# RG-LRU loop of a hybrid diffusion block: width-4 convolution and gates on the products in PSUM, zero columns around the context, another order of the products

## The chip, the cores and the metric

The kernel runs on one core of one Trainium2 chip. The metric is the device time of one execution in microseconds.

## The reference

One layer works on 512 latent tokens (`x`) and 256 context tokens (`ctx`), 1024 channels each, in fp32. The part that matters here is the recurrent branch of the token mixer. Its input `x_r` is a projection of the normalised and modulated tokens. It goes through a depthwise convolution of width 4 (latent and context tokens apart, with zero padding of one token before and two after), and then for each of two directions through gates and a linear recurrence that runs over the context first:

```
xr = dwconv1d(xr, lru_conv_w, (1, 2)) + lru_conv_b
for d in range(2):
    r = sigmoid(heads(xr) @ w_r[d] + b_r[d]);  i = sigmoid(heads(xr) @ w_i[d] + b_i[d])
    log_a = -8 * r * softplus(-lam[d]);        a = exp(log_a)
    u = sqrt(-expm1(2 * log_a)) * (i * xr)
    h = scan(h = a * h + u), latent tokens start from the last context state; d = 1 runs backwards
    rec = h if d == 0 else rec + h
```

`rec` times a GeLU gate is projected, merged with a Conformer branch (GLU, depthwise convolution of width 31, LayerNorm, projection), and followed by an output projection and a gated ConvFFN.

## The kernel before, in words

Channels lie on the partitions, tokens on the columns. The 1024 channels of a branch are 8 blocks of 128. Every fp32 operand of a product is split into a high and a low float32r part, and a product is three matmuls (`mm3`, L134 to 137). A product of a block over 512 tokens (`block`, L143) is 24 matmuls. Weights come by DMA from the SP queue in a fixed order (`queue`, `W`, L94 to 132). ScalarE makes a weight's high part (L123), GpSimd its low part (L124). `W` converts two entries ahead of the one that is asked for. The order on every engine is the order of the calls in the program: the schedule is manual, and each engine's queue is strictly in order.

The loop over the blocks (L640 to 699) is software pipelined. In iteration b TensorE computes x_r of block b, the gates of block b-1, and the g and v products of block b+1 for the GLU. VectorE and GpSimd do the scans of block b-2. The tiles of the products lie in PSUM under tags: `mm2` (two buffers of 1024 columns, for x_r, the gates, and gelu blocks 4 and 5), `mm1` (two of 512, for g, v and the other gelu blocks) and `cv` (two of 512). A buffer is given out again in rotation, and the first writer waits until all readers of the tile before have run.

- `xr_post` (L539): ScalarE copies x_r from PSUM into a zero-padded SBUF tile `xrp` (latent at 1, context at 515; L541, L542), and makes the first tap `xw` from it (L545). VectorE adds two taps over 770 columns (L547), with a fill after each, and the last tap in two pieces (L550, L552) into `xc`.
- `xc_split` (L556): high part on ScalarE, low part on GpSimd (helper `split`, L140, L141).
- `gates` (L562): two products, of r and of i, of direction d. `gates_act` (L583): ScalarE takes the tanh of both from PSUM into SBUF tiles `tg` (L580), then a = exp (L589) and a second tanh (L590). GpSimd squares a into `e2` (L592; the page and the trace call it `e`).
- `gates_dve` (L595): the input-gate product (L598) and the r product (L600), both from SBUF.
- `scans_act` (L602): square roots (L605), which need another activation table. `scans` (L607): the scan product (L610), by VectorE for direction 0 and by GpSimd for direction 1; three scans (L614 to 616); the sum of the directions on GpSimd (L617).
- `fill(n)` (L532) hands out n operations of the width-31 convolution (`conv31`, L484, taps at L500) to VectorE. What the loop leaves is done by the next stage, before the LayerNorm's mean (L788 to 792).
- `ada_step` (L289) adds a product of the adaLN modulation, two per iteration in b = 2 to 5, from tiles loaded in the same iteration (L673 to 676). `decay_rates` (L370) is a chain of small GpSimd operations before the loop.

Before the loop the products of block 0 are made into `psA` and `psC`, `psg` is g of block 2 and `ps1` is x_r of block 1 (L473 to 476). After it (L701 to 722) follow the gates of block 7, the scans of blocks 6 and 7 and the gelu blocks (`gt_block`, `gt_act`, L622 to 629), then the stage of the gb and yb products (L750).

## Time and profile before

| | us |
|---|---|
| median of three runs | 909.12 |
| the three runs | 909.12, 909.26, 906.13 |
| span of the profiled execution, first to last instruction | 906.8 |
| TensorE matmul busy | 860.2 |
| VectorE busy | 723.3 |
| GpSimd busy | 476.6 |
| ScalarE busy | 440.3 |

The profile gives the span of one execution, not its time as the runs count it; that is the span and what lies around it. Engines are PE (TensorE), DVE (VectorE), ACT (ScalarE), POOL (GpSimd) and SP. A row names line, engine, operation, and "out<-in" by the program's names. The time of the RG-LRU loop is from about 73 to 276 us. PEclk is TensorE's granted clock as a share of full speed. Matmuls overlap, so the time of a product is read from start to start. A "[1.34 <-ACT ...]" behind a row is the engine's idle time before it and what ended it.

### The profile page before, as it was taken

How to read it: one execution, taken by the hardware profiler on the slowest of the kernel's cores; microseconds unless marked ns; L12 is line 12 of the kernel's file. 1: busy time of each engine (PE TensorE's matmuls, PEld its weight loads, DVE VectorE, ACT ScalarE, POOL GpSimd, SP SyncE). 2: the span in 40 equal slices, each digit the busy share in tenths (PEclk: the TensorE clock that was granted, in tenths of full speed). 3: DMA queues.
4: the chain of work that ended last, by engine and by line, in shares of the span. 5: the costliest groups of instructions: out<-in, count | busy, mean ns of one | idle time of the engine just before them, and what ended most of it. 6: DMA issues, size and time to landing. Idle time of an engine off the chain costs nothing.

```text
span 906.8 us, 11008 instructions
## 1 busy us (share of the span) xinstructions
PE 860.2 (95%) x4114; PEld 692.0 (76%) x4114; DVE 723.3 (80%) x952; ACT 440.3 (49%) x625; POOL 476.6 (53%) x263
## 2 busy tenths in 40 slices
PE   7999989888989999999898999999999999999997
PEld 6787777766867768887676788988888888888775
DVE  4387999999999888885888334699999898899314
ACT  5285656654678455422654245544443443435322
POOL 2229667555766499955344213254554564547810
PEclk9999999988999989999999899999999999999999
DMA  9942133213212222324425322133333333233402
GB/s 351 367 195 82 35 128 128 94 52 111 82 47 94 93 71 96 113 94 163 160 82 177 124 108 70 48 105 116 124 101 122 116 119 116 91 130 116 163 1 93
DMA packets 31397, 105.97 MB, mean 117 GB/s; under 512 B 3441, under 2 KB 3569, under 8 KB 31345
## 3 DMA queue, kind: packets, MB, share of 16 engines
q1 hardware_dynamic: 31344, 105.29, 33.8%
q8 instruction: 32, 0.52, 0.2%
q14 instruction: 21, 0.16, 0.1%
HBM read 103.17 MB, written 2.10 MB: 116 GB/s over the span
## 4 chain that ended last, share of the span: by engine, by line
PE 60%; DVE 29%; ACT 5%; DMA 3%; issue 3%; POOL 1%; SPq 0%; DVEq 0%; ACTq 0%; POOLq 0%
PE up_ps L136 8%; PE up_ps L135 8%; PE up_ps L137 8%; DVE cv L500 6%; DVE xw L547 3%; DVE tg L598 3%; DVE e L600 3%; DVE ggb L294 2%; PE y_ps L135 2%; PE y_ps L137 2%; PE y_ps L136 2%; PE gb_ps L137 2%; DVE rec L615 2%; PE gb_ps L135 1%; PE gb_ps L136 1%
## 5 line engine op out<-in xcount | busy, mean ns | idle before, releaser
L124 POOL TENSOR_TENSOR wlo<-raw,whi 128x1024 fp32r<-128x1024 f32 (+1 forms) x126 | 314.4, 2508 | 200.5 <-ACT whi L123 198.0
L1016 DVE SCALAR_TENSOR_TENSOR cv<-zall,P,cv 128x512 f32<-128x512 f32 x240 | 161.7, 741 | 0.2
L500 DVE SCALAR_TENSOR_TENSOR cv<-glu,P,cv 128x512 f32<-128x512 f32 x208 | 141.5, 746 | 0.0
L123 ACT ACTIVATE whi<-raw 128x1024 fp32r<-128x1024 f32 (+1 forms) x129 | 129.5, 1023 | 16.4 <-issue 10.9
L135 PE MATMUL up_ps<-Ahi,whi 128*128 128x512 f32 (+1 forms) x352 | 131.9, 375 | 0.0
L136 PE MATMUL up_ps<-Alo,whi 128*128 128x512 f32 (+1 forms) x352 | 131.8, 374 | 0.0
L137 PE MATMUL up_ps<-Ahi,wlo 128*128 128x512 f32 (+1 forms) x352 | 131.7, 374 | 0.0
L136 PEld LDWEIGHTS up_ps<-Alo,whi 128*128 128x128 f32 x352 | 66.1, 188 | 13.2
L137 PEld LDWEIGHTS up_ps<-Ahi,wlo 128*128 128x128 f32 x352 | 66.1, 188 | 13.2
L135 PEld LDWEIGHTS up_ps<-Ahi,whi 128*128 128x128 f32 x352 | 66.1, 188 | 13.1
L1002 POOL TENSOR_TENSOR acl<-fo,ach 128x512 fp32r<-128x512 f32 x20 | 26.0, 1301 | 85.5 <-ACT ach L999 85.5
L1016 DVE SCALAR_TENSOR_TENSOR cv<-zall,P,cc 128x512 f32<-128x512 f32 x40 | 43.1, 1104 | 21.1 <-ACT cc L990 21.1
L988 ACT ACTIVATE zall<-up_ps 128x512 f32<-128x512 f32 x40 | 23.7, 593 | 63.3 <-PE up_ps L137 63.3
L999 ACT ACTIVATE ach<-fo 128x512 fp32r<-128x512 f32 x20 | 12.7, 633 | 66.8 <-DVE fo L998 66.8
L294 DVE SCALAR_TENSOR_TENSOR ggb<-wa,sT,ggb 128x1024 f32<-128x1024 f32 (+1 forms) x35 | 43.7, 1249 | 0.4
L135 PE MATMUL gate_ps<-xh,whi 128*128 128x512 f32 x64 | 24.1, 376 | 17.8 <-ACT xrp L542 17.7
L547 DVE SCALAR_TENSOR_TENSOR xw<-xrp,P,xw 128x770 f32<-128x770 f32 x16 | 33.7, 2107 | 2.1 <-ACT xw L545 2.0
L135 PEld LDWEIGHTS gate_ps<-xh,whi 128*128 128x128 f32 x64 | 13.0, 203 | 22.7 <-ACT xrp L542 20.1
L598 DVE SCALAR_TENSOR_TENSOR tg<-tg,xc 128x768 f32<-128x768 f32 x16 | 30.2, 1885 | 0.0
L605 ACT ACTIVATE e<-e 128x768 f32<-128x768 f32 x16 | 13.5, 846 | 33.9 <-DVE e L600 33.8
L617 POOL TENSOR_TENSOR rec<-rec,tg 128x512 f32<-128x512 f32 x7 | 9.2, 1311 | 36.6 <-DVE tg L616 36.6
L580 ACT ACTIVATE tg<-gate_ps,P 128x768 f32<-128x768 f32 x32 | 27.4, 898 | 2.0 <-PE gate_ps L137 1.8
(386 smaller groups left out, 2245.9 us busy)
## 6 DMA issues: line engine op xcount, KB each, us to landing
raw<-in_win_dram SPq DMA_DIRECT2D x48, 512.0 KB, 3.4
raw<-in_wup_dram SPq DMA_DIRECT2D x40, 512.0 KB, 3.3
wa<-in_wada_dram SPq DMA_DIRECT2D x24, 512.0 KB, 5.5
raw<-in_wdn_dram SPq DMA_DIRECT2D x22, 512.0 KB, 3.3
wa<-in_wadq_dram SPq DMA_DIRECT2D x16, 512.0 KB, 9.3
raw<-in_wpl_dram SPq DMA_DIRECT2D x8, 512.0 KB, 3.2
raw<-in_wpc_dram SPq DMA_DIRECT2D x8, 512.0 KB, 3.3
raw<-in_wout_dram SPq DMA_DIRECT2D x8, 512.0 KB, 3.3
```

Of the source, the lines that this page charges most:

```text
L123: S.activation(out=flat(hl[0]), in_=flat(t), func=AF.Copy)
L124: eng.tensor_sub(flat(hl[1]), flat(t), flat(hl[0]))
L135: PE.matmul(o, lh, rh, start=first, stop=False)
L136: PE.matmul(o, lh, rl, start=False, stop=False)
L137: PE.matmul(o, ll, rh, start=False, stop=last)
L294: V.scalar_tensor_tensor(out=acc, in0=w, scalar=s, in1=acc, op0=ALU.mult, op1=ALU.add)
L500: V.scalar_tensor_tensor(out=cv[b] if k else glu[:, b, 0:T], in0=glu[:, b, k:k + T], scalar=col("dw31", 31 * b + k, 1), in1=cv[b], op0=ALU ...
L547: V.scalar_tensor_tensor(out=xw, in0=pad[:, k:k + 770], scalar=lw[k], in1=xw, op0=ALU.mult, op1=ALU.add)
L580: S.activation(out=t, in_=lru[b, d, q][:, 0:TA], func=AF.Tanh, scale=0.5, bias=hb[:, 16 * q + i:16 * q + i + 1])
L598: V.scalar_tensor_tensor(out=ti, in0=ti, scalar=1.0, in1=xcs[b][0], op0=ALU.add, op1=ALU.mult)
L600: V.scalar_tensor_tensor(out=e2, in0=e2, scalar=1.0, in1=tr, op0=ALU.add, op1=ALU.mult)
L1016: V.scalar_tensor_tensor(out=o, in0=zz[i, s][:, k // 3:k // 3 + GH, k % 3:k % 3 + GW], scalar=col("dw9", 9 * (i + FW * (1 - s)) + k, 1), i ...
```

## The change

The context's products are made over 262 columns, with three zero columns on either side of `chi` and `clo`, so that the x_r product lies in PSUM with its own zero padding. The copies into `xrp` go. ScalarE makes the second tap with the bias straight from PSUM (`xr_act`), and VectorE adds the other three with PSUM as one operand (`xr_post`). The tanh of the gates, and the second tanh of r, are written in place in PSUM. The input-gate product goes into a new tile `u`, and the r product reads PSUM. The backward and forward scans write into `e2`. Gate weights get buffers of their own (`gw`). In the loop the four gate products are taken apart: r of direction 0 after the context product; i of direction 0 and r of direction 1 after g (or a gelu block); i of direction 1 after v. The part behind the loop is reordered in the same way, and squares for block 7 move from VectorE to GpSimd. The loop's fills are 82 (90 before), and those behind it 6 (10 before). Comments are dropped too.

```diff
+TP = TC + 6
...
-    chi = ph.tile([128, NB, TC], F32R, name="chi")
-    clo = ph.tile([128, NB, TC], F32R, name="clo")
+
+    chi = ph.tile([128, NB, TP], F32R, name="chi")
+    clo = ph.tile([128, NB, TP], F32R, name="clo")
+    for t in (chi, clo):
+        for sl in (slice(0, 3), slice(3 + TC, TP)):
+            G.memset(t.bitcast(F32)[:, :, sl] if hasattr(t, "bitcast") else t[:, :, sl], 0.0)
     w0h = ph.tile([128, NB, 128], F32R, name="w0h")
     w0l = ph.tile([128, NB, 128], F32R, name="w0l")
+
+    def gate_dst():
+        return tuple(ph.tile([128, 4, 128], F32R, tag=f"gw{n}", bufs=2, name=f"gw{n}") for n in "hl")
...
-        queue(("gate", b - 1), wgate[b - 1], [4, 128])
+        queue(("gate", b - 1), wgate[b - 1], [4, 128], gate_dst)
...
-        split(h, chi[:, k:k + 2, :], clo[:, k:k + 2, :])
+        split(h, chi[:, k:k + 2, 3:3 + TC], clo[:, k:k + 2, 3:3 + TC])
...
-    block(psA[:, T:TA], ready[0], chi, clo)
+    block(psA[:, T:T + TP], ready[0], chi, clo)
...
-    def xr_post(b, ps, n=1):
-        pad = xrp[b % 2]
-        S.activation(out=pad[:, 1:1 + T], in_=ps[:, 0:T], func=AF.Copy)
-        S.activation(out=pad[:, 515:515 + TC], in_=ps[:, T:TA], func=AF.Copy)
+
+    def xr_act(b, ps):
+        xw = pl.tile([128, 771], F32, tag="xw", bufs=1, name="xw")
+        S.activation(out=xw, in_=ps[:, 0:771], func=AF.Identity, scale=col("lru_w", 4 * b + 1, 1),
+                     bias=col("lru_b", b, 1))
+        return xw
+
+    def xr_post(b, ps, xw, n=1):
         lw = [col("lru_w", 4 * b + k, 1) for k in range(4)]
-        xw = pl.tile([128, 770], F32, tag="xw", bufs=1, name="xw")
-        S.activation(out=xw, in_=pad[:, 0:770], func=AF.Identity, scale=lw[0], bias=col("lru_b", b, 1))
-        for k in (1, 2):
-            V.scalar_tensor_tensor(out=xw, in0=pad[:, k:k + 770], scalar=lw[k], in1=xw, op0=ALU.mult, op1=ALU.add)
-            fill(n)
+        V.scalar_tensor_tensor(out=xw[:, 1:771], in0=ps[:, 0:770], scalar=lw[0], in1=xw[:, 1:771], op0=ALU.mult, op1=ALU.add)
+        fill(n)
+        V.scalar_tensor_tensor(out=xw, in0=ps[:, 1:772], scalar=lw[2], in1=xw, op0=ALU.mult, op1=ALU.add)
+        fill(n)
         xc = pl.tile([128, TA], F32, tag="xc", name="xc")
-        V.scalar_tensor_tensor(out=xc[:, 0:T], in0=pad[:, 3:3 + T], scalar=lw[3], in1=xw[:, 0:T],
-                               op0=ALU.mult, op1=ALU.add)
-        V.scalar_tensor_tensor(out=xc[:, T:TA], in0=pad[:, 517:517 + TC], scalar=lw[3], in1=xw[:, 514:770],
-                               op0=ALU.mult, op1=ALU.add)
+        for o, w in ((0, T), (T, TC)):
+            i = o + 3 * (o > 0)
+            V.scalar_tensor_tensor(out=xc[:, o:o + w], in0=ps[:, i + 2:i + 2 + w], scalar=lw[3], in1=xw[:, i:i + w],
+                                   op0=ALU.mult, op1=ALU.add)
         xcs[b] = xc
...
-    def gates(b, d, mid=None):
+
+    def gate_mm(b, d, q):
         _, xh, xl = xcs[b]
         gh, gl = ready[index["gate", b]]
-        for q in range(2):
-            ps = mm2("gate_ps")
-            for a0, a1 in ((0, T), (T, TA)):
-                mm3(ps[:, a0:a1], gh[:, 2 * d + q, :], gl[:, 2 * d + q, :], xh[:, a0:a1], xl[:, a0:a1], True, True)
-            lru[b, d, q] = ps
-            if mid and q == 0:
-                mid()
-
-    def gates_tanh(b, d):
+        ps = mm2("gate_ps")
+        for a0, a1 in ((0, T), (T, TA)):
+            mm3(ps[:, a0:a1], gh[:, 2 * d + q, :], gl[:, 2 * d + q, :], xh[:, a0:a1], xl[:, a0:a1], True, True)
+        lru[b, d, q] = ps[:, 0:TA]
+
+    def gate_tanh(b, d, q):
+        i = 16 * q + 8 * d + b
+        S.activation(out=lru[b, d, q], in_=lru[b, d, q], func=AF.Tanh, scale=0.5, bias=hb[:, i:i + 1])
+
+    def r_act(b, d):
+        gate_tanh(b, d, 0)
         i = 8 * d + b
-        for q in range(2):
-            if (b, d) == (7, 0):
-                t = pl.tile([128, D], F32, tag="wa", name="tg")[:, 0:TA]
-            else:
-                t = pl.tile([128, TA], F32, tag=f"tg{q}", name=f"tg{q}")
-            S.activation(out=t, in_=lru[b, d, q][:, 0:TA], func=AF.Tanh, scale=0.5, bias=hb[:, 16 * q + i:16 * q + i + 1])
-            lru[b, d, q] = t
-
-    def gates_act(b, d):
-        if (b, d) != (7, 0):
-            gates_tanh(b, d)
-        i = 8 * d + b
-        tr, ti = lru[b, d, 0], lru[b, d, 1]
-        a = pl.tile([128, TA], F32, tag="a", name="a")
+        tr = lru[b, d, 0]
+        a = pl.tile([128, TA], F32, tag="a", bufs=3, name="a")
         S.activation(out=a, in_=tr, func=AF.Exp, scale=nshalf[:, i:i + 1], bias=nshalf[:, i:i + 1])
         S.activation(out=tr, in_=tr, func=AF.Tanh, scale=shalf[:, i:i + 1], bias=shalf[:, i:i + 1])
         e2 = pl.tile([128, TA], F32, tag="e2", name="e2")
-        (V if b == 7 else G).tensor_mul(e2, a, a)
+        G.tensor_mul(e2, a, a)
         lru[b, d] = (a, e2)
 
-    def gates_dve(b, d):
-        tr, ti = lru[b, d, 0], lru[b, d, 1]
-        a, e2 = lru[b, d]
-        V.scalar_tensor_tensor(out=ti, in0=ti, scalar=1.0, in1=xcs[b][0], op0=ALU.add, op1=ALU.mult)
-        fill(1)
-        V.scalar_tensor_tensor(out=e2, in0=e2, scalar=1.0, in1=tr, op0=ALU.add, op1=ALU.mult)
+    def r_dve(b, d):
+        e2 = lru[b, d][1]
+        V.scalar_tensor_tensor(out=e2, in0=e2, scalar=1.0, in1=lru[b, d, 0], op0=ALU.add, op1=ALU.mult)
+
+    def i_dve(b, d):
+        u = pl.tile([128, TA], F32, tag="u", name="u")
+        V.scalar_tensor_tensor(out=u, in0=lru[b, d, 1], scalar=1.0, in1=xcs[b][0], op0=ALU.add, op1=ALU.mult)
+        lru[b, d, 1] = u
 
...
-        hf, hb = lru[b, 0, 0], lru[b, 1, 0]
+        hf, hb = [lru[b, d][1] for d in range(2)]
...
-    xr_post(0, psA, 0)
+    xr_post(0, psA, xr_act(0, psA), 0)
     xc_split(0)
-    pend, gp = None, {}
+    pend = None
     for b in range(1, NB):
         w = W(("xr", b))
         if b == 1:
@@ -644,85 +643,93 @@
         else:
             ps = mm2("xr_ps")
             block(ps[:, 0:T], w, Ahi, Alo)
-        if b >= 2:
             scans_act(b - 2)
-        block(ps[:, T:TA], w, chi, clo)
+        block(ps[:, T:T + TP], w, chi, clo)
         if pend is not None:
             glu_mul(*pend)
             pend = None
         if b >= 2:
             scans(b - 2)
-        fill(6)
+        fill(3)
         W(("gate", b - 1))
-        def g_part():
-            gp[0] = mm1("g_ps")
-            block(gp[0], ready[index["g", b + 1]], Ahi, Alo, (0,))
-
-        gates(b - 1, 0, g_part if 1 < b < NB - 1 else None)
+        gate_mm(b - 1, 0, 0)
+        xw = xr_act(b, ps)
+        r_act(b - 1, 0)
         if b in (2, 6):
             rest = ada_cols(2 + b // 6, ggb, mm1("ada_cp"))
-        xr_post(b, ps)
-        gates_act(b - 1, 0)
         if b == 1:
             tg = gate_act(psg)
         elif b + 1 < NB:
-            block(gp[0], W(("g", b + 1)), Ahi, Alo, range(1, NB))
-            tg = gate_act(gp[0])
+            gps = mm1("g_ps")
+            block(gps, W(("g", b + 1)), Ahi, Alo)
         else:
             gt_block(0)
+        xr_post(b, ps, xw)
+        if b in (2, 6):
+            rest()
+        fill(2)
+        r_dve(b - 1, 0)
+        xc_new = xcs.pop(b)
+        gate_mm(b - 1, 0, 1)
+        gate_mm(b - 1, 1, 0)
+        if 1 < b < NB - 1:
+            tg = gate_act(gps)
+        gate_tanh(b - 1, 0, 1)
+        r_act(b - 1, 1)
+        i_dve(b - 1, 0)
         if 2 <= b <= 5:
             for k in (2 * b - 4, 2 * b - 3):
                 was[k] = pl.tile([128, D], F32, tag="wa", name="wa")
                 nc.sync.dma_start(out=was[k], in_=wada[1, :, k, :])
-        if b == 1:
+        if b + 1 < NB:
             psv = mm1("v_ps")
-            block(psv, W(("v", 2)), Ahi, Alo, range(4))
-        gates(b - 1, 1)
-        if b in (2, 6):
-            rest()
-        gates_dve(b - 1, 0)
-        gates_act(b - 1, 1)
-        xc_split(b)
-        fill(2 if b < 7 else 0)
-        if b + 1 < NB:
-            if b > 1:
-                psv = mm1("v_ps")
-            block(psv, W(("v", b + 1)), Ahi, Alo, range(4 if b == 1 else 0, NB))
+            block(psv, W(("v", b + 1)), Ahi, Alo)
             pend = (tg, psv, b + 1)
         else:
             gt_block(1)
-        gates_dve(b - 1, 1)
         if 2 <= b <= 5:
             for k in (2 * b - 4, 2 * b - 3):
                 ada_step(k, was[k], ggb)
-        elif b < 7:
+        else:
             fill(4)
+        fill(3)
+        r_dve(b - 1, 1)
+        gate_mm(b - 1, 1, 1)
+        gate_tanh(b - 1, 1, 1)
+        xcs[b] = xc_new
+        xc_split(b)
+        i_dve(b - 1, 1)
 
     W(("gate", 7), 2)
+    scans_act(NB - 2)
+    gate_mm(7, 0, 0)
+    r_act(7, 0)
+    scans(NB - 2)
+    gt_block(2)
     gt_act(0)
     gt_act(1)
-    gates(7, 0)
-    gates_tanh(7, 0)
-    scans_act(NB - 2)
-    scans(NB - 2)
-    gt_block(2)
-    gates_act(7, 0)
     fill(2)
-    gates(7, 1)
+    r_dve(7, 0)
+    gate_mm(7, 0, 1)
+    gate_mm(7, 1, 0)
+    gate_tanh(7, 0, 1)
+    r_act(7, 1)
+    i_dve(7, 0)
     gt_block(3)
-    fill(6)
-    gates_act(7, 1)
-    gates_dve(7, 0)
+    fill(4)
+    r_dve(7, 1)
+    gate_mm(7, 1, 1)
+    gate_tanh(7, 1, 1)
+    i_dve(7, 1)
+    scans_act(7)
+    gt_block(4)
     gt_act(2)
     gt_act(3)
-    gt_block(4)
-    gates_dve(7, 1)
-    scans_act(7)
     gt_block(5)
     scans(7)
     es_r.close()
```

## Rows read from the trace of the kernel before

**Rows 1.** The page, part 4: the chain that ended last, by engine.
```profile
PE 60%; DVE 29%; ACT 5%; DMA 3%; issue 3%; POOL 1%; SPq 0%; DVEq 0%; ACTq 0%; POOLq 0%
```

**Rows 2.** Table by stretch, one block: length; busy PE, PEld, DVE, ACT, POOL; PEclk, DMA.
```profile
162.74:192.70 29.96, 25.93 (x118) 21.03 (x118) 29.86 (x28) 17.90 (x21) 18.43 (x9) 0.90 0.28 97
```

**Rows 3.** Groups by shape of VectorE, 103.76 to 251.29 us: busy us, mean ns.
```profile
L547 DVE SCALAR_TENSOR_TENSOR xw<-xrp,P,xw 128x770 f32<-128x770 f32 x10 | 22.7, 2269 | 0.0
L598 DVE SCALAR_TENSOR_TENSOR tg<-tg,xc 128x768 f32<-128x768 f32 x10 | 20.1, 2013 | 0.0
...
L353 DVE SCALAR_TENSOR_TENSOR glu<-tg,v_ps 128x512 f32<-128x512 f32 x5 | 3.4, 676 | 0.0
```

**Rows 4.** Timelines of GpSimd and VectorE: start, duration, instruction, idle before.
```profile
277.44 2.27 POOL L610 TENSOR_TENSOR tg<-tg,e 128x768 f32<-128x768 f32 x1 [1.77 <-ACT e L605]
...
278.12 2.68 DVE L615 TENSOR_TENSOR_SCAN rec<-a,tg,tg 128x512 f32<-128x512 f32 x1
```

**Rows 5.** Timeline of VectorE: the first scan of block 4 and the fills behind the scans.
```profile
224.21 0.69 DVE L614 TENSOR_TENSOR_SCAN tg<-a,tg 128x256 f32<-128x256 f32 x1
...
227.79 4.02 DVE L500 SCALAR_TENSOR_TENSOR cv<-glu,P,cv 128x512 f32<-128x512 f32 x6
```

**Rows 6.** Who waited for whom, 67 to 310 us: total us, times, longest.
```profile
PE gate_ps L135 <- ACT xrp L542: 17.7, 6, 4.0
```

**Rows 7.** Timeline of ScalarE in one block.
```profile
201.52 1.04 ACT L123 ACTIVATE whi<-raw 128x1024 fp32r<-128x1024 f32 x1
...
202.95 1.68 ACT L580 ACTIVATE tg<-gate_ps,P 128x768 f32<-128x768 f32 x2
...
209.33 0.85 ACT L140 ACTIVATE xh<-xc 128x768 fp32r<-128x768 f32 x1 [2.72 <-DVE xc L552]
...
211.67 1.28 ACT L605 ACT_TABLE_LOAD   x1
212.96 0.85 ACT L605 ACTIVATE e<-e 128x768 f32<-128x768 f32 x1
```

**Rows 8.** Timeline of GpSimd: a weight's low part, and xc's.
```profile
229.21 2.42 POOL L124 TENSOR_TENSOR wlo<-raw,whi 128x1024 fp32r<-128x1024 f32 x1
...
240.20 1.86 POOL L141 TENSOR_TENSOR xl<-xc,xh 128x768 fp32r<-128x768 f32 x1 [1.91 <-ACT xh L140]
```

**Rows 9.** Timeline of TensorE: first product of x_r, its context part, r0, g.
```profile
92.11 0.40 PE L135 MATMUL xr_ps<-Ahi,whi 128*128 128x512 f32 x1
...
97.71 0.28 PE L135 MATMUL xr_ps<-chi,whi 128*128 128x256 f32 x1
...
100.59 0.39 PE L135 MATMUL gate_ps<-xh,whi 128*128 128x512 f32 x1
...
101.64 0.39 PE L135 MATMUL g_ps<-Ahi,whi 128*128 128x512 f32 x1
```

**Rows 10.** Table by stretch (columns of rows 2), after waits of 3.4 and 1.3 us.
```profile
220.80:227.20 6.40, 5.81 (x20) 4.03 (x21) 6.33 (x6) 2.47 (x4) 0.82 (x1) 0.50 0.00 0
103.80:107.80 4.00, 3.96 (x23) 2.91 (x24) 3.93 (x6) 1.41 (x2) 0.18 (x1) 1.00 0.01 4
```

**Rows 11.** Timelines of TensorE and VectorE at the loop's start and end.
```profile
71.95 0.39 PE L135 MATMUL xr_ps<-Ahi,whi 128*128 128x512 f32 x1
...
73.36 2.07 DVE L547 SCALAR_TENSOR_TENSOR xw<-xrp,P,xw 128x770 f32<-128x770 f32 x2
...
267.70 0.50 PE L135 MATMUL gate_ps<-xh,whi 128*128 128x512 f32 x1 [0.17 <-ACT xh L140]
```

**Rows 12.** Timelines of ScalarE and TensorE after the loop: first Gelus; second gb.
```profile
270.86 1.09 ACT L628 ACTIVATE ge<-gt_ps 128x512 f32<-128x512 f32 x2
...
326.33 0.80 PE L137 MATMUL gb_ps<-Ahi,wlo 128*128 128x512 f32 x1 [0.56 <-POOL wlo L124]
```

**Rows 13.** Timelines of VectorE and TensorE: last taps of conv31; product of the sums.
```profile
414.91 1.40 DVE L500 SCALAR_TENSOR_TENSOR glu<-glu,P,cv 128x512 f32<-128x512 f32 x2
...
425.72 1.02 PE L792 MATMUL mean<-lnsum,mones 128*128 128x512 f32 x2
```

More of the change, by code (lines that the diff above doesn't have):

```diff
@@ L186, in backbone_kernel @@
         if b == 1:
-            queue(("gate", 7), wgate[7], [4, 128])
+            queue(("gate", 7), wgate[7], [4, 128], gate_dst)
     for b in range(NB):
@@ L210, in norm_a @@
         ss = st.tile([128, 1], F32, tag="ss", name="ss")
-        S.activation(out=junk, in_=slot, func=AF.Square, accum_out=ss)
+        S.activation(out=junk, in_=slot if len(junk.shape) == 2 else slot.rearrange("p (a b) -> p a b", b=junk.shape[2]),
+                     func=AF.Square, accum_out=ss)
         r = rstd_of(ss, "x")
@@ L229, in backbone_kernel @@
         S.activation(out=sT[:, :, v:v + 1], in_=col(nm).unsqueeze(2), func=AF.Silu)
-    xrp = []
-    for i in range(2):
-        t = ph.tile([128, 773], F32, name=f"xrp{i}")
-        G.memset(t, 0.0)
-        xrp.append(t)
     adl = const.tile([128, 48], F32, name="adl")
@@ L422, in backbone_kernel @@
     for t in range(2):
-        norm_a(None, xc_tok[t], flat(clo[:, 4 * t:4 * t + 4, :]))
+        norm_a(None, xc_tok[t], clo[:, 4 * t:4 * t + 4, 3:3 + TC])
     pre = st.tile([128, 1], F32, tag="sd", name="pre")
```

## Prediction

> **What bounds the kernel now.** I read the page's chain first: TensorE holds 60% of it and VectorE 29% [rows 1], so one asks where the VectorE share lies. The table by stretch answers: in one block of the RG-LRU loop VectorE is busy for 29.86 of 29.96 us, while TensorE, whose products of a block need far less, ran at a mean granted clock of 0.90 [rows 2]. So the loop is VectorE's. The groups by shape say why: the two middle taps (L547) average 2.27 us for 770 columns and the input-gate product (L598) 2.01 us for 768, but the GLU product (L353), with one operand in PSUM, stays at 0.68 us for 512 [rows 3]. The two timelines side by side give the cause of the spread: a scan (L615) that needs 1.28 us took 2.68, and ended its wait just where a GpSimd product (L610, 277.44 + 2.27 = 279.71) ended [rows 4]. Operations with both tensors in SBUF wait for GpSimd's whole instruction; those with one in PSUM don't.
>
> **Part 1, cheaper VectorE work.** The change puts one operand of the taps, of the input-gate product and of the r product (L600) into PSUM. The new operations are not in the trace. Below, 0.87 us (a free L598: 0.94 long, and 0.87 to the next start); above, 2.27, L547's mean with its waits [rows 3]. I take 0.87, because L353, the nearest form (one PSUM operand, SBUF result), shows no wait at all: its mean times 770/512 is 1.0 with the overlap of neighbours still in it. Per block that is 2 x 1.4 for the taps and 2 x 1.1 for L598, and two fewer conv31 taps ("fills", 0.67 each, six in 4.02 us [rows 5]) give 1.3: over 6 us of VectorE time per block. ScalarE loses two copies of 0.58 and 0.37 us; it waits often, so I give nothing for them alone.
>
> [...] L353's 0.68 us for 512 columns shows no surcharge for a PSUM operand [rows 3]. [...]
>
> **Part 2, what it lengthens.** In the kernel before, TensorE waits in the loop for one thing that counts: the ScalarE copies that free the x_r product's PSUM, 17.7 us in six waits [rows 6]. After, the two 1024-column PSUM buffers alternate through x_r, r0, i0, r1, i1 (r, i gates of directions 0 and 1). So i0 waits until VectorE's whole width-4 convolution has read x_r, r1 until the r product of direction 0 is done, and i1 and the next blocks follow. The next block's path starts at ScalarE's tanh of i1: behind it are queued, in order, the copy of xc, a weight split, the square roots with a table load, and behind those VectorE's scans and convolution. I walk that circle from the end of i1 on TensorE (t = 0):
> - ScalarE: tanh 0.85, xc copy 0.75, weight split 0.95, load 1.3, root 0.85, read from start to start: 4.7 [rows 7].
> - The first scan product (L610, direction 0) is ready at 4.7 but has both tensors in SBUF. GpSimd starts xc's low part at 1.6, 1.85 us, then a weight's low part, 2.4 us [rows 8]: port free at 5.85. The product ends at 6.7.
> - GpSimd takes its own scan product then, 1.8 us (1.63 to 2.27 in rows 4): 8.5. The scans, 3.6 us from L614's start to the fills [rows 5]: 12.1.
> - Three fills 2.0: 14.1. Convolution: two taps 1.74, two fills 1.33, last tap 1.05 (in two pieces): 18.2. TensorE, with 5.6 + 2.95 + 1.05 + 5.6 us of x_r (262 columns now), r0 and g [rows 9], was free at 15.2: it waits 3.0 for i0.
> - Two fills and the r product: 20.4; r1 could start at 19.3: 1.1 more. r1 1.05, v 5.6, i1 1.05: 28.15.
>
> So a block takes 28.15 us at full clock. Before, it is from x_r of block 2 at 92.11 [rows 9] to the first product of block 7's gates at 267.70 [rows 11] six blocks, 29.27 each. Gain 6 x 1.1 = 6.7 us, though VectorE idles nearly 8 us per block: its saving goes off the path. The two adaLN loads of a block are issued behind a weight load that waits for GpSimd; their sums have some 1.5 us of cover on VectorE, and I cost them at nothing; without it the next x_r waits as long.
>
> **Clock.** [...] Half of 5.81, 2.9 us, is the upper price, nothing the lower. In the loop 1.05 of it, i0's slower half, is hidden under the r product, so 0 to 1.85, taken half: 6 x 0.9 = +5.4. The loop's net is -1.3.
>
> **Part 3, start.** Copies of block 0's x_r freed its buffer early; now the convolution reads it. It starts at 73.36 behind the GLU products [rows 11], and 0.87 + 0.87 + 0.66 + 0.45 brings it to 76.2, so x_r of block 1 starts there and not at 71.95 [rows 11]. Then 5.6 + 2.95 = 84.75; copy 0.85, convolution with two fills 4.1, i0 at 89.85; two fills and r product 92.0; r1, v, i1: 99.75, where TensorE was at 92.11 before: +7.6. Two waits of 4 us follow each other there (71.95 to 76.2, 85.8 to 89.85), and I add half the price of a low stretch, 1.4: +9.0.
>
> **Part 4, tail.** The product of gelu block 2 needs the buffer of block 0, whose Gelu on ScalarE now stands behind the last block's r activations: 4.7 + 0.75 (second root), load 1.3, tanh, exp, tanh 2.7, split 0.95, load 1.3, Gelu 0.55: 12.2 after the loop's end. Before, the Gelus came first [rows 12]. From there six gelu products, three gates, and the first gb and yb make 33.6 + 3.15 + 11.2 = 48: the second gb starts at 60.2. Before it is 267.70 to 326.33 [rows 11, 12], 58.6: +1.6, and 1.4 again for the clock: +3.0. GpSimd makes e2 ahead of its scan product there, which holds the last scan, but TensorE is later still.
>
> **Part 5, fills.** The loop does 88 in place of 100; 12 x 0.67 = 8 us go to the next stage, where VectorE ended at 416.3 and TensorE asked for the sums at 425.72 [rows 13]. With GpSimd's last two additions (2.5) that is 426.2 or so: +0.5. The zero columns' memsets replace others at the start: nothing, hidden by the input loads.
>
> **Sum.** 9.0 - 1.3 + 3.0 + 0.5 = +11.2 us. The profiled span is 906.8; the three runs shown are 906.1 to 909.3 with a median of 909.1, 2.3 above the span, which I take as what lies around it. Forecast 920.3 us. About 0.5%, 4.5 us, is what a measurement of this kernel can tell from no change.
>
> **Rivals.**
> 1. The clock stays up (waits 3.0 and 1.1, near the edge of rows 10). For it: the 1.3 us wait cost no clock. Against: 3.0 is nearer 3.4. Then 7.6 - 6.7 + 1.6 + 0.5 = +3.0: 912.1, no change.
> 2. Faster: the scan products and scans don't meet GpSimd. The place is the 1.15 and 1.8 us at the head of the circle; without both a block is 25.2, the waits of TensorE vanish, and 6 x (25.2 - 29.27) = -24.4, with 7.6 + 1.6 + 0.5: -14.7, 894.4 us. It decides from a block time under 26.9 us, where six blocks give back the 9.7 of the other parts and 4.5 more. For: scans of the loop before were all free of waits. Against: there GpSimd was idle, and in the walk it is not.
> 3. Each low stretch is the long one: loop +4.4, start 10.5, tail 4.5, with 0.5: +19.9, 929 us.
> 4. The change doesn't do what it says: PSUM operands wait for GpSimd as before. Three operations on the circle at 2.0 in place of 0.87 add 3.4 per block, 20 us in six: 941 us. L353 speaks against it.
>
> **Chances.** Forecast 0.41; rival 1 0.16; rival 2 and its halves 0.28; rival 3 0.11; rival 4 0.04. So slower 0.56, same 0.16, faster 0.28. The forecast's own range is 914 to 928. The range of 8 in 10 takes in most of rival 2 and rival 3: 895 to 929.
>
> **What would show it.** Right: r and i products and taps near 0.95 us whatever GpSimd does; VectorE with several us idle per block, released by ScalarE's root and by tanh of i1; TensorE waiting for VectorE's last tap before i0, some 3 us, for it again before x_r of block 1 (4 us), and for Gelu near the loop's end (7 us); block times of 28 to 30 us. Wrong: block times near 25 with TensorE without gaps (rival 2), or a granted clock of 1.00 throughout the loop (rival 1).

## The result and the profile after

The changed kernel takes 922.1 us (median of four runs, 920.3 to 923.6) against 909.2 for the kernel before in the same session: a ratio of 1.0151, 95% interval 1.0126 to 1.0176. It is slower, by 12.9 us where 11.2 were forecast. The profiled run has a span of 921.5 us.

The page of the changed kernel, part 1 in part and part 4 in part, answers to [rows 1]:

```profile
PE 865.8 (94%) x4114; PEld 699.4 (76%) x4114; DVE 689.0 (75%) x950; ACT 433.3 (47%) x609; POOL 460.9 (50%) x267
...
PE 71%; DVE 17%; ACT 8%; issue 2%; DMA 1%; POOL 1%; DVEq 0%; SPq 0%; POOLq 0%; ACTq 0%
```

VectorE's share of the chain fell from 29% to 17%, and the time went up all the same. The table by stretch shows why that is no contradiction. Here are the iterations b = 2 to 7 of the loop, called blocks 2 to 7 below, with the columns of [rows 2]:

```profile
101.38:132.09 30.71, 28.21 (x133) 22.82 (x132) 23.27 (x27) 17.12 (x19) 16.86 (x9) 0.89 0.26 93
132.09:161.01 28.92, 25.77 (x123) 21.26 (x122) 23.30 (x25) 17.12 (x19) 17.31 (x9) 0.94 0.25 86
161.01:190.74 29.73, 25.78 (x122) 21.18 (x121) 23.42 (x25) 17.11 (x19) 16.87 (x9) 0.94 0.30 104
190.74:220.91 30.17, 27.01 (x123) 22.27 (x122) 23.31 (x25) 17.11 (x19) 16.86 (x9) 0.89 0.27 103
220.91:251.59 30.68, 28.17 (x132) 22.77 (x131) 23.86 (x29) 17.11 (x19) 16.88 (x9) 0.89 0.17 55
251.59:282.39 30.80, 25.91 (x123) 21.18 (x121) 24.25 (x28) 18.21 (x21) 16.91 (x9) 0.94 0.18 61
```

VectorE is busy for 23.3 us of a block and no longer for 29.9 [rows 2], yet a block lasts about 30 us. No engine is full. The timeline of VectorE in the block that starts at 132.09 shows how the time passes:

```profile
133.19 0.96 DVE L598 SCALAR_TENSOR_TENSOR u<-gate_ps,xc 128x768 f32<-128x768 f32 x1 [3.88 <-ACT gate_ps L579]
134.07 0.68 DVE L356 SCALAR_TENSOR_TENSOR glu<-tg,v_ps 128x512 f32<-128x512 f32 x1
137.06 1.97 DVE L609 TENSOR_TENSOR u<-u,e 128x768 f32<-128x768 f32 x1 [2.31 <-ACT e L604]
139.07 2.21 DVE L613 TENSOR_TENSOR_SCAN e<-a,u 128x256 f32<-128x256 f32 x1
...
144.16 2.05 DVE L503 SCALAR_TENSOR_TENSOR cv<-glu,P,cv 128x512 f32<-128x512 f32 x3
146.12 1.02 DVE L551 SCALAR_TENSOR_TENSOR xw<-xr_ps,P,xw 128x770 f32<-128x770 f32 x1
...
149.29 1.14 DVE L558 SCALAR_TENSOR_TENSOR xc<-xr_ps,P,xw 128x512 f32<-128x512 f32 x2
150.34 1.40 DVE L503 SCALAR_TENSOR_TENSOR cv<-glu,P,cv 128x512 f32<-128x512 f32 x2
151.66 0.95 DVE L594 SCALAR_TENSOR_TENSOR e<-e,gate_ps 128x768 f32<-128x768 f32 x1
```

VectorE idles 3.88 us until the tanh of i1 and 2.31 until the root, then loses 1.0 and 1.5 us behind GpSimd in the first scan product (L609; 0.95 where GpSimd leaves it alone, see the last section) and the first scan (L613; 0.69 in [rows 5]). Three fills, the taps, two fills and the r product (L594) follow in its queue. TensorE waits for the last tap before i0; its timeline in the same block, and the waits of TensorE from 60 to 310 us (total, times, longest), show that this happens in each block:

```profile
150.57 0.77 PE L136 MATMUL gate_ps<-xh,gwh 128*128 128x512 f32 x1 [3.15 <-DVE xc L558]
```

```profile
PE gate_ps L136 <- DVE xc L558: 22.1, 7, 4.5
```

These 22.1 us in seven waits stand where the kernel before had 17.7 in six [rows 6].

### The profile page after: what moved, and what is told of

It reads as the page before. It is cut to its first block, busy times and chain, and to the rows that moved or that the text cites. A ratio compares the mean times of both kernels' runs of the same rounds, so it can differ in the third digit from the quotient of the medians.

```text
span 921.5 us, 11017 instructions
## 1 busy us (share of the span) xinstructions
PE 865.8 (94%) x4114; PEld 699.4 (76%) x4114; DVE 689.0 (75%) x950; ACT 433.3 (47%) x609; POOL 460.9 (50%) x267
## 4 chain that ended last, share of the span: by engine, by line
PE 71%; DVE 17%; ACT 8%; issue 2%; DMA 1%; POOL 1%; DVEq 0%; SPq 0%; POOLq 0%; ACTq 0%
PE up_ps L137 8%; PE up_ps L136 8%; PE up_ps L138 8%; DVE cv L503 4%; PE gate_ps L136 2%; PE yb_ps L138 2%; PE yb_ps L136 2%; PE yb_ps L137 2%; PE gb_ps L137 2%; PE gb_ps L136 2%; PE gb_ps L138 2%; PE y_ps L137 2%; PE y_ps L136 2%; PE y_ps L138 2%; PE v_ps L136 2%
## 5 line engine op out<-in xcount | busy, mean ns | idle before, releaser
L125 POOL TENSOR_TENSOR wlo<-raw,whi 128x1024 fp32r<-128x1024 f32 x118 | 291.1, 2476 | 197.2 <-ACT whi L124 197.2
L124 ACT ACTIVATE whi<-raw 128x1024 fp32r<-128x1024 f32 x121 | 125.4, 1051 | 16.5 <-issue 10.9
L579 ACT ACTIVATE gate_ps<-gate_ps,P 128x768 f32<-128x768 f32 x32 | 28.0, 875 | 77.9 <-PE gate_ps L138 75.5
L136 PE MATMUL gate_ps<-xh,gwh 128*128 128x512 f32 x64 | 28.5, 445 | 24.6 <-DVE xc L558 22.1
L589 POOL TENSOR_TENSOR e<-a 128x768 f32<-128x768 f32 x16 | 24.0, 1497 | 51.9 <-ACT a L586 48.9
L598 DVE SCALAR_TENSOR_TENSOR u<-gate_ps,xc 128x768 f32<-128x768 f32 x16 | 15.3, 957 | 36.0 <-ACT gate_ps L579 36.0
L297 DVE SCALAR_TENSOR_TENSOR ggb<-wa,sT,ggb 128x1024 f32<-128x1024 f32 (+1 forms) x35 | 39.5, 1128 | 0.4
L136 PEld LDWEIGHTS gate_ps<-xh,gwh 128*128 128x128 f32 x64 | 15.2, 237 | 30.8 <-issue 24.9
L136 PE MATMUL gt_ps<-Ahi,whi 128*128 128x512 f32 x64 | 26.2, 409 | 7.0 <-ACT ge L627 7.0
L609 DVE TENSOR_TENSOR u<-u,e 128x768 f32<-128x768 f32 x9 | 15.6, 1743 | 18.0 <-ACT e L604 18.0
```

What stands on the lines that cost most here:

```text
L124: S.activation(out=flat(hl[0]), in_=flat(t), func=AF.Copy)
L125: eng.tensor_sub(flat(hl[1]), flat(t), flat(hl[0]))
L136: PE.matmul(o, lh, rh, start=first, stop=False)
L297: V.scalar_tensor_tensor(out=acc, in0=w, scalar=s, in1=acc, op0=ALU.mult, op1=ALU.add)
L579: S.activation(out=lru[b, d, q], in_=lru[b, d, q], func=AF.Tanh, scale=0.5, bias=hb[:, i:i + 1])
L589: G.tensor_mul(e2, a, a)
```

## The experiments

The theory: a block is as long as a circle of waits, which runs through the in-order queues of ScalarE and VectorE and the two large PSUM buffers. The rivals: the low clock, the handover of x_r's buffer alone, VectorE's work.

**Is it the clock?** Dummy products fill TensorE's waits.

```diff
+        if b + 1 < NB:
+            psv = mm1("v_ps")
+            warm(psv, 14)
         gate_mm(b - 1, 0, 1)
+        if b + 1 < NB:
+            warm(psv, 4)
         gate_mm(b - 1, 1, 0)
...
-            psv = mm1("v_ps")
```

> The changed kernel, with dummy products on TensorE (14 small ones ahead of gate i0, 4 ahead of gate r1, into the PSUM buffer of the next v product) that fill its waits, so that its granted clock need not fall after them; they add work to TensorE and leave nothing out. Theory (circle): the waits stay in length, but the products behind them run at the full clock; the block falls from 30.2 us to the walked 28.2 to 28.7, time 910 to 915 us, best guess 913. Rival (the low clock is the whole loss): 905 to 910, the time before or below it. Rival (TensorE's work sets the block): the dummies add up to 3 us to a block, 930 or more.

Measured: 921.1 us, ratio to the kernel before 1.0141 (1.0122 to 1.0159), so the total hardly moved. The table by stretch of this kernel, blocks 2 to 6, same columns:

```profile
96.84:130.16 33.32, 30.84 (x169) 26.18 (x167) 23.18 (x27) 17.12 (x19) 16.86 (x9) 0.95 0.25 84
130.16:158.55 28.39, 28.35 (x158) 24.28 (x157) 23.32 (x25) 17.11 (x19) 16.91 (x9) 1.00 0.29 103
158.55:186.96 28.41, 28.38 (x159) 24.31 (x158) 23.30 (x25) 17.12 (x19) 16.88 (x9) 1.00 0.29 102
186.96:215.36 28.40, 28.36 (x159) 24.28 (x157) 23.33 (x25) 17.11 (x19) 16.92 (x9) 1.00 0.30 104
215.36:247.04 31.68, 29.20 (x168) 24.55 (x167) 23.86 (x29) 17.11 (x19) 16.86 (x9) 1.00 0.19 56
```

In blocks 3 to 5 the clock stays at 1.00 and a block takes 28.40 us three times over: the walked 28.15 within 0.25. So the circle is there with the clock up, and the clock is worth 29.6 - 28.4 = 1.2 us in such a block on average (0.5, 1.3 and 1.8 in the three). Blocks 2 and 6 got longer, because there the dummies themselves waited (2.48 us, for the adaLN copies to free their PSUM buffer): they gave back the 3.6 us that blocks 3 to 5 had won, and the total missed the expectation mainly for that reason. The clock as the whole cause falls.

**Is it VectorE's queue?** The seven fills of the circle go elsewhere.

```diff
+            fill(3)
             scans(b - 2)
-        fill(3)
...
-        xr_post(b, ps, xw)
+        xr_post(b, ps, xw, 0)
...
-        fill(2)
         r_dve(b - 1, 0)
...
         xc_split(b)
+        fill(4)
         i_dve(b - 1, 1)
```

> The changed kernel, with the 7 fills (steps of the 31-wide convolution, about 0.64 us each) that stand ahead of the convolution's last tap and of the r product moved to places where VectorE is idle in every block; nothing is left out. Theory (a circle of waits through VectorE's in-order queue and the two large PSUM buffers sets the block, not an engine's work): the last tap ends 3.2 us and the r product 4.5 us sooner, TensorE's waits before i0 and r1 (3.2 and up to 0.8 us) go, the clock stays up, and a block falls from 30.2 us to TensorE's own 25 to 26.5; time 885 to 905 us, best guess 893. Rival, VectorE's work sets the block: it has 23.6 us of work per block and the work is the same, so the time stays at 920 to 924. Rival, the handover of x_r's buffer to i0 alone: i0 is released sooner by 3.2 us per block, about 902.

Measured: 901.2 us, ratio 0.9927 (0.9899 to 0.9955): 21 us under the changed kernel with the same work. The table by stretch, and TensorE's waits from 60 to 310 us:

```profile
126.05:152.75 26.70, 24.47 (x120) 20.23 (x120) 21.96 (x26) 16.43 (x19) 17.52 (x10) 1.00 0.30 95
152.75:178.44 25.69, 24.48 (x121) 20.24 (x121) 21.48 (x26) 16.09 (x19) 16.96 (x9) 1.00 0.33 114
```

```profile
PE gt_ps L136 <- ACT ge L627: 7.5, 1, 7.5
PE xr_ps L136 <- DVE e L594: 6.7, 4, 2.6
PE gate_ps L136 <- DVE e L594: 4.6, 6, 1.6
PE gate_ps L136 <- ACT tg L352: 3.4, 1, 3.4
```

No product waits for the last tap any more. Waits of 0.3 to 2.6 us for the r product (L594) came in their place, so that a block takes 25.4 to 29.1 us, and the time missed the best guess by 8 us while staying in its range. VectorE's work as the bound falls: the same work fits into 25.7 us. The handover rival does not fall here: 901.2 is close to its 902, and the next run has to part it from the theory.

**Is it the handover of x_r's buffer alone?** A copy of x_r frees it early.

```diff
+        xp = pl.tile([128, 774], F32, tag="xp", bufs=1, name="xp")
+        S.activation(out=xp[:, 0:773], in_=ps[:, 0:773], func=AF.Copy)
         xw = pl.tile([128, 771], F32, tag="xw", bufs=1, name="xw")
-        S.activation(out=xw, in_=ps[:, 0:771], ...
+        S.activation(out=xw, in_=xp[:, 0:771], ...
...
```

The three taps read `xp` too, and block 0's weight tiles `w0h` and `w0l` lie in another pool.

> The changed kernel, with x_r copied by ScalarE from PSUM into SBUF at once, and the convolution reading the copy; nothing is left out, one ScalarE copy of about 0.9 us per block is added. Theory (circle through VectorE's queue): i0 no longer waits, but r1 then waits about 3 to 4 us for the r product, which stands behind the convolution in VectorE's queue and now comes about 1 us later; the block gets 0 to 2 us longer, time 922 to 934 us, best guess 928. Rival (the handover of x_r's PSUM buffer to i0 is what costs): TensorE's 3.2 us per block go, time 899 to 906. Rival (reading the convolution's operands in PSUM is what pays): slower by over 10 us, since the taps contend with GpSimd again.

Measured: 951.1 us, in a single run. VectorE's groups by shape from 103 to 282 us (busy, mean ns), and a wait of TensorE from 95 to 300 us:

```profile
L554 DVE SCALAR_TENSOR_TENSOR xw<-xp,P,xw 128x770 f32<-128x770 f32 x5 | 12.8, 2556 | 0.0
```

```profile
PE gate_ps L136 <- DVE e L597: 44.4, 6, 7.9
```

i0 no longer waits, and r1 waits 7 to 8 us instead, for the r product that must free r0's buffer. VectorE's first tap is back at 2.56 us with both inputs in SBUF, and it, the next one and the larger piece of the last take 3.5 us more per block together. I had expected the move of the wait but only half its size, since I left the slower taps to a rival: both are at work. Without these 3.5 us and the copy's 0.9, r1 would still wait some 3 us (an estimate), as long as i0 did before: the handover alone is not what costs.

**Which part of the change costs?** The PSUM convolution and the padded context alone, in the kernel before: its `gates`, `gates_tanh` and the order of its loop stay, `xr_post` and the context tiles are those of the change.

> The kernel before, with the PSUM convolution and the padded context alone (old order of products, gates as before); nothing is left out. Theory (the order of the products belongs to the PSUM convolution, for the x_r buffer now is held until the last tap): the second gate product stands in front of the g product and waits for the last tap, behind scans and 8 fills, so a block grows from 29.3 to 34 to 40 us; time 940 to 975 us, best guess 955. Rival (cheaper VectorE work decides, since VectorE is busy for 29.2 of a block's 29.3 us before): the block falls to TensorE's 25 to 27 us, 880 to 897.

Measured: 904.9 us in a single run; timed again:

> The same kernel as in the look at the PSUM convolution alone, timed in rounds; nothing is left out. That look gave 904.9 us and overturned the expectation (940 to 975): gate i0 took the buffer of r0, which a tanh into SBUF frees after 0.9 us, so it did not wait for the last tap. Theory now (the PSUM convolution alone is worth a little, and gates that stay in PSUM, holding both large buffers until VectorE's r and i products, cost the rest): 903 to 907 us, a ratio of 0.993 to 0.998. Rival (the look was a stray and this part costs time too): 909 or more.

904.3 us, ratio 0.9966 (0.9952 to 0.9981). The timeline of TensorE shows where my expectation went wrong:

```profile
106.76 0.50 PE L136 MATMUL gate_ps<-xh,whi 128*128 128x512 f32 x1 [2.92 <-ACT tg L582]
```

i0 waits for a tanh and not for the last tap. With a tanh that carries r0 out of PSUM at once, r0's buffer is the first to come free, and i0 takes that one, although the last tap stands ahead of that tanh in the program. So x_r may be held until the last tap at little cost. The complement, then: the order of the change, but gates whose tanh writes to SBUF.

```diff
+        t = pl.tile([128, TA], F32, tag=f"tg{q}", name=f"tg{q}")
-        S.activation(out=lru[b, d, q], in_=lru[b, d, q], func=AF.Tanh, ...
+        S.activation(out=t, in_=lru[b, d, q], func=AF.Tanh, ...
+        lru[b, d, q] = t
...
-        u = pl.tile([128, TA], F32, tag="u", name="u")
+        u = lru[b, d, 1]
```

`w0h` and `w0l` lie in another pool here too, and in the two kernels below that are built on this one.

> The changed kernel (same order of products, same fills, PSUM convolution), but with the gates' first tanh writing to SBUF tiles, as in the kernel before, so that a gate's PSUM buffer is free after one tanh; the r and i products read SBUF again. Nothing is left out. Theory (what costs is that gates in PSUM hold both large buffers until VectorE's queue comes to the r and i products): i0 takes r0's buffer and does not wait, r1 waits 1 to 3 us for the last tap, a block falls from 30.2 to 27.5 to 29 us, time 906 to 915, best guess 911. Rival (the place of the convolution and its fills in VectorE's queue is all): i0 or r1 waits as long as before, and contention adds 0.5 to 1 us to a block: 922 to 930.

Measured: 907.0 us in a single run, 15 us under the changed kernel. The table by stretch and the wait that is left in the loop, for r1 (95 to 300 us):

```profile
151.77:179.58 27.81, 25.76 (x122) 21.42 (x121) 24.36 (x26) 17.58 (x19) 17.89 (x9) 0.94 0.29 103
179.58:207.40 27.82, 25.75 (x122) 21.43 (x121) 23.93 (x26) 17.59 (x19) 17.92 (x9) 0.94 0.30 102
```

```profile
PE gate_ps L136 <- DVE xc L558: 11.5, 6, 2.5
```

So gates that stay in PSUM cost here: they hold both large buffers until VectorE's queue comes to the r and i products. They do not cost by themselves, since the kernel with the moved fills keeps them in PSUM and takes 901.2 us. It is the hold together with seven fills ahead of its end in VectorE's queue, and taking away either one wins back the time.

**Versions that beat both.** In the kernel with the moved fills, two waits were left at the loop's ends. Behind the loop two Gelus, gt2 and gt3 come forward, and five eighths of a v product ahead of block 0's i0.

```diff
         gate_tanh(b - 1, 1, 1)
+        if b == NB - 1:
+            gt_act(0)
+            gt_act(1)
...
     W(("gate", 7), 2)
+    gt_block(2)
     scans_act(NB - 2)
     gate_mm(7, 0, 0)
     r_act(7, 0)
     scans(NB - 2)
-    gt_block(2)
-    gt_act(0)
-    gt_act(1)
+    gt_block(3)
...
```

> The kernel with the moved fills (901.2 us) and two more moves of work, nothing left out: behind the loop the first two Gelus and the products gt2 and gt3 come forward into TensorE's waits (1.7 + 1.4 us for block 7's xh and xl, 7.5 us for the Gelu), and in block 0 five of the v product's eight parts come ahead of i0, which waited 3.4 us. Theory (each wait filled is worth its length less what turns up behind it): tail 5 to 7 us, start 1 to 3 us, time 892 to 896, best guess 894. Rival (the waits only move, since r1 and i1 of block 7 then wait for VectorE): 898 to 902.

Measured: 900.3 us, ratio 0.9920 (0.9894 to 0.9946), no different from 901.2. The rival holds: the Gelu's wait fell from 7.5 to 2.9 us, and waits of 2.7 us for r products appeared behind it. In block 0, x_r of block 2 now waits 3.0 us for the r product.

The move of the fills and the move behind the loop were then made with gates that leave PSUM, in two steps.

> The order of the changed kernel, with its gates' tanh into SBUF (907.0 us in one look) and with the 7 fills moved as in the first experiment; nothing is left out. Theory (two holds were left: the gates' buffers, freed by a tanh here, and x_r's buffer, which r1 waits for 1.4 to 2.5 us per block until the last tap): the taps end about 3 us sooner, r1 no longer waits, no other product waits for VectorE, a block falls from 28 to 25.5 to 26.5 us; time 891 to 898, best guess 895. Rival (VectorE, 86% busy in that loop and reading gates from SBUF beside GpSimd, is the next bound): 900 to 906.

Measured: 901.9 us, ratio 0.9929 (0.9901 to 0.9957): the rival. Blocks still take 27.8 us and r1 still waits 2.0 us for the taps:

```profile
147.79:175.58 27.79, 25.76 (x123) 21.41 (x121) 25.25 (x26) 17.58 (x19) 18.29 (x9) 0.94 0.32 104
```

VectorE has little idle time left there (25.25 of 27.79 us busy), so the moved fills delay the scans: the second one starts 12.3 us after x_r's first product (132.30 - 120.01) where it was 9.7 without the move (133.23 - 123.52), and the taps behind them end only 0.5 us sooner (18.4 us after x_r's first product, 18.8 without the move). What was won against the single run of 907.0 lies ahead of block 3: from block 0's context product to block 3's x_r it took 56.2 us in place of 61.6.

> The same, and behind the loop the first two Gelus, gt2 and gt3 come forward into TensorE's waits (1.7 + 1.4 + 7.8 us there). With the gates in PSUM this move gave back nearly all, because r1 and the next product then waited 2.7 us each for VectorE's r products. Theory (that give-back was the hold again): with gates that a tanh frees, the move is worth 4 to 7 us on the kernel without it, time 886 to 892, best guess 890. Rival (the stage behind, whose products and 31-wide convolution steps are what they were, takes it back anyway): within 1.5 us of the kernel without the move.

Measured: 899.4 us (896.0 to 903.9), ratio 0.9880 (0.9839 to 0.9921). The gain of 2.6 us lies between theory and rival, within the spread of the runs: not settled.

The better start was the kernel with the PSUM convolution alone. Four of g's eight parts go between r0 and i0, where TensorE waited for r0's tanh.

```diff
-            block(gp[0], ready[index["g", b + 1]], Ahi, Alo, (0,))
+            block(gp[0], ready[index["g", b + 1]], Ahi, Alo, range(4))
...
-            block(gp[0], W(("g", b + 1)), Ahi, Alo, range(1, NB))
+            block(gp[0], W(("g", b + 1)), Ahi, Alo, range(4, NB))
```

> The kernel with the PSUM convolution alone in the old order (904.9 us in one look), where i0 waits 2.4 to 3.4 us per block for r0's tanh; now four of the g product's eight parts stand between r0 and i0 instead of one, so 2.6 us more of other work covers that wait. Nothing is left out or added. Theory (a wait of TensorE that is covered by its own later work is won back): 2 to 2.5 us per block for 5 blocks, 10 to 12 us, time 891 to 897, best guess 894, with VectorE's 27.3 us per block as the next bound. Rival (VectorE, 93% busy in that loop, sets the block): at most 3 us, 901 to 905.

Measured: 896.8 us, ratio 0.9889 (0.9856 to 0.9922): 7.4 us won of the 10 to 12 expected. The table by stretch of its loop, and what TensorE waited for, show what came next:

```profile
92.40:232.40 140.00, 127.14 (x621) 103.60 (x620) 137.30 (x145) 88.52 (x99) 97.36 (x46) 0.98 0.27 94
```

```profile
PE gate_ps L136 <- ACT tg L582: 9.1, 8, 2.4
PE gate_ps L136 <- DVE xc L554: 7.1, 3, 2.4
```

The tanh's waits halved (18.8 us in the kernel without the move), and VectorE, busy for 137.3 of 140.0 us, looked like the bound. So the last kernel takes work from it in the loop:

```diff
-        xr_post(b, ps, xr_act(b, ps))
+        xr_post(b, ps, xr_act(b, ps), 0)
```

> The kernel with the PSUM convolution, the old order and four parts of g between r0 and i0 (896.8 us), with the two fills between the convolution's taps left to the later stage: 14 fewer fills (0.65 us each) in the loop, 14 more behind it; nothing is left out. VectorE is busy for 137.3 of 140.0 us of that loop, and r1 waits up to 2.4 us for the last tap. Theory (VectorE's work is the bound there now, and behind the loop it has 10.5 us to spare before the LayerNorm's mean): 1.3 us per block, 7 to 9 us, time 887 to 892, best guess 889. Rival (the later stage pays the fills back, or GpSimd contention takes the place): 895 to 899.

Measured: 896.2 us, ratio 0.9861 (0.9844 to 0.9877), the rival. The first gb product starts 1.4 us sooner (296.6 for 298.0), and the product of the LayerNorm's sums 2.0 us later (415.2 for 413.2), now with a wait for the sums:

```profile
  POOL lnsum L512: 1.6, 1
```

Part of the gain was paid back behind the loop. The gain itself was small: in the same five blocks VectorE had 9 us less of fills (43.4 to 34.4), but was busy for only 5 us less (132.3 us), and the time fell by 2.1 us (137.9 for 140.0). Its other operations got longer, as the rival's second half has it; that GpSimd is the reason was not tested. Both of these kernels beat the kernel before by over 1% (1.1 and 1.4).

## Why the prediction was right, and which of its steps were off

**Cheaper VectorE work off the path: right.** The two long taps take 1.01 us on average, and the r and i products 0.946 to 0.958 us in all 32 cases, whatever GpSimd does; the rival in which PSUM operands still wait for GpSimd falls. The page's groups show what became of the time won, in the idle time before these two:

```profile
L598 DVE SCALAR_TENSOR_TENSOR u<-gate_ps,xc 128x768 f32<-128x768 f32 x16 | 15.3, 957 | 36.0 <-ACT gate_ps L579 36.0
...
L609 DVE TENSOR_TENSOR u<-u,e 128x768 f32<-128x768 f32 x9 | 15.6, 1743 | 18.0 <-ACT e L604 18.0
```

**No surcharge for PSUM: right for these products.** The r product with an operand in PSUM lasts 0.949 us on average, the same product with both in SBUF 0.94 to 0.95 us where GpSimd leaves it alone (0.95 and 0.94 in the kernel before at 187.89 and 247.79, 0.95 in the kernel whose gates leave PSUM at 124.23).

**The circle: right in length, wrong in one reason.** i0 waited 2.5 to 3.2 us (3.0 walked), a block with the clock up (at 1.00) takes 28.40 (28.15 walked), and the first scan product and scan met GpSimd as walked; the rival without that meeting falls. But the step "the two 1024-column PSUM buffers alternate" put the wait on the convolution's hold of x_r. The runs show that hold to be harmless by itself (904.3 us); it cost here because the gates hold the other buffer (922.1 with that hold, 907.0 without) and the fills delay the release (901.2 without them). Buffers are not given out in turns, as the prediction and the description of the kernel before have it: in each case that was read, the product took the buffer that came free first (i0 that of r0 where a tanh frees it, that of x_r in the changed kernel; x_r of block 1 that of the GLU products). By which rule the framework chooses is not shown.

**The loop's sum: the term that failed.** From x_r of block 2 to the end of block 6's i1, at 280.67, it took 179.3 us where 6 x 29.05 = 174.3 were forecast: +3.7 against the kernel before instead of -1.3. The step that failed is above all the clock, put at 0.9 us in every block. Of these 5.0 us, 4.4 lie in blocks 2, 5 and 6. There the granted clock was 0.50 to 0.53 for 6.4 us behind i0's wait, as in the long stretch of [rows 10], while in blocks 3, 4 and 7 it averaged 0.73 to 0.75 over such a stretch. Block 2, behind a wait of only 2.50 us, with the columns of [rows 2]:

```profile
120.20:126.60 6.40, 6.40 (x17) 5.14 (x18) 5.26 (x7) 2.63 (x3) 0.83 (x1) 0.50 0.62 235
```

So the upper price of 1.85 us was paid about where the clock stayed low (1.8 in block 5), the loop came near the +4.4 of the rival in which each low stretch is the long one, and the length of the wait did not decide it: blocks 3, 4, 5 and 7 all waited 3.15 to 3.17 us. The forecast's terms for the clock (0.9 us in a block, 1.4 at the start and in the tail) are shares of half of 5.81 us [rows 10], an estimate that no run shows; in place of the 0.9 the runs showed 0.5, 1.3 and 1.8 us in blocks 3 to 5. Blocks 2 and 6 also hold adaLN copies that I had left out: two more TensorE products (0.64 and 0.38 us) and two more steps in VectorE's queue (0.42 and 0.16). No run parts the two there.

**The start: +7.5 us, forecast +9.0.** The step "x_r of block 1 starts" when block 0's convolution frees its buffer failed: it took the buffer of the GLU products and waited 1.4 us. Then block 0's i0 waited 4.5 us for the taps (4.0 walked), which kept most of the sum. The walk to i0 also adds up to 89.7 and not 89.85.

```profile
75.30 0.50 PE L136 MATMUL xr_ps<-Ahi,whi 128*128 128x512 f32 x1 [1.37 <-DVE glu L356]
```

**The tail: +5.4, forecast +3.0.** gt2 starts 12.5 us after the loop's end (12.2 walked), and the second gb 62.4 us after it (61.6 with the clock's share). But the start of the second gb before was misread: the row at 326.33 in [rows 12] is the third matmul of that product. The first one starts at 324.71, so that the stretch before was 57.0 us and not 58.6, and the walk's own terms give +4.6.

```profile
293.17 0.79 PE L136 MATMUL gt_ps<-Ahi,whi 128*128 128x512 f32 x1 [7.03 <-ACT ge L627]
...
343.07 0.40 PE L136 MATMUL gb_ps<-Ahi,whi 128*128 128x512 f32 x1
```

and in the kernel before:

```profile
324.71 0.63 PE L135 MATMUL gb_ps<-Ahi,whi 128*128 128x512 f32 x1
```

**The fills: the wait came, the sum did not.** TensorE waited 0.32 us for the sums, which it did not before; half a microsecond was forecast, though the terms given (416.3 + 8 + 2.5 = 426.8) make +1.1. Yet the stretch from the second gb to the product of the sums is 98.7 us, 101.0 before: -2.3, because the second gb itself, which took 8.5 us before, at a low clock (0.50 over its first 4.29 us) and with a wait of 0.56 us for a low part, took 5.6 (at 1.00). The rest of the program took 1.3 us less.

**Not foreseen.** In the profiled run block 0's context product starts at 65.03, 1.8 us later than before. That is this run and not the change: the kernel with the moved fills has the same code up to there, and starts it at 63.11. The changed kernel, the kernel before, and the one with the moved fills:

```profile
65.03 0.28 PE L136 MATMUL xr_ps<-chi,w0h 128*128 128x262 f32 x1
```

```profile
63.23 0.28 PE L135 MATMUL xr_ps<-chi,w0h 128*128 128x256 f32 x1
```

```profile
63.11 0.28 PE L136 MATMUL xr_ps<-chi,w0h 128*128 128x262 f32 x1
```

So 1.8 + 7.5 + 3.7 + 5.4 - 2.3 - 1.3 = 14.8, the difference of the two spans (14.7). Against the forecast that is -1.5 at the start, +5.0 in the loop, +2.4 in the tail, -2.8 behind it, and +1.8 and -1.3 elsewhere. The start and the tail made the kernel slower as forecast; the loop, where a gain was forecast, lost. That the time came within 2 us is in part luck, since these misses, which sum to 3.6 us, partly cancel.

## What to carry to other kernels

Work taken from the busiest engine can be worth nothing, as here, if the new form makes a buffer wait for that engine's queue: before keeping an operand in PSUM, list who must read it before its buffer comes free, and where those readers stand in their queue. In a circle of waits, work moved out of the queue ahead of the releaser into true idle time is won (21 us here); filling the wait with other products of the waiting engine won 7.4 us where a tanh was the releaser, and nothing where VectorE's queue only released the next product later. Test the parts of a change one by one: here one of them was a gain, and with two lines of new order it gave the better kernel.

## What the runs showed of the hardware that was not expected

The clock fell after the wait before i0 in every block (to 0.50 to 0.75 on average over the next 6.4 us), but waits of one length cost differently. After the 3.15 us of block 3 the granted clock was 0.75 on average over the next 6.43 us of full work (0.50 over the first 3.23 us, 0.99 over the other 3.20), and 1.00 after that; after the 3.16 us of block 5, and after the 2.5 us of blocks 2 and 6, it was 0.50 to 0.53 over 6.40 us. With the wait filled by dummy products it stayed at 1.00 through three blocks. The rows of the changed kernel, block 3:

```profile
150.57:157.00 6.43, 6.43 (x24) 5.30 (x25) 5.22 (x6) 3.24 (x4) 1.50 (x2) 0.75 0.66 255
157.00:160.00 3.00, 3.00 (x15) 2.41 (x14) 3.00 (x5) 0.91 (x2) 2.83 (x2) 1.00 0.01 3
```

And the meeting of VectorE and GpSimd is a matter of a microsecond: in the kernel with the moved fills, where the first scan product starts after GpSimd's low part, it and the first scan take 0.95 and 0.69 us instead of 1.97 and 2.21.

```profile
158.69 0.95 DVE L609 TENSOR_TENSOR u<-u,e 128x768 f32<-128x768 f32 x1
159.68 0.69 DVE L613 TENSOR_TENSOR_SCAN e<-a,u 128x256 f32<-128x256 f32 x1
```
